# Operand addresses at multiples of 512 bytes, and the last three attention-branch panels after all gates

## The chip, the cores and the metric

The kernel runs on one core of a Trainium2 chip. The metric is the device time of one execution in microseconds (us). TensorE (PE) multiplies, VectorE (DVE), ScalarE (ACT) and GpSimd (POOL) work on tiles, and DMA queues, most of them issued from SyncE (SP), move data.

## The reference, cut to what matters

One block on 512 tokens of width 2048, all in float32:

```
h = rms_norm(x);  q, k, v, u, ga, gb = split(h @ w_in)         # 16 heads of 64
yA = chunked attention(q, k, v, clipped relative bias)         # width 1024
yB = multi-scale causal pooling(u) @ pool_w * pool_scale       # width 1024
m  = sigmoid(ga) * (yA @ w_branch_a) + sigmoid(gb) * (yB @ w_branch_b)
x1 = x + m @ w_out
out = rms_norm(x1 + (silu(g) * up) @ w_down),  g, up = split(rms_norm(x1) @ w_gate_up)
```

## The kernel before

**Precision.** A float32 operand is split in two float32r parts, a high part (an ACT copy) and a low part (a DVE subtraction). One product is three matmuls: low x high, high x high, high x low. A matmul has a stationary operand of 128 x 128 values (512 bytes in each partition), loaded by a LDWEIGHTS, and a moving one of 512 columns (2048 bytes in each partition; 256 columns for v).

**First half, panels.** `panel` (lines 204 to 206) computes 256 output columns of one weight matrix. Weights come in units of 4 x 256 columns: `load_to` issues the DMA into a `raw` tile (L143), `hi_to` splits off the high part on ACT (L152), `lo_to` the low part on DVE (L161); all three kinds lie in the pool `stage`, three tiles each. The unit is stationary, the activations move: `XH`/`XL` in the pool `xhl` (the normed input, 16 + 16 tiles), `ybh`/`ybl` and later `yah`/`yal` in the pool `mid`. In `panel_v` (L410 to L412) `XH`/`XL` are stationary and the weights move. Two more users of matmuls, pooling's small products and the attention scores, take both operands from the pool `slots`. The order is q, k, v, u, then the gb gates with the pooling-branch panels, then for i = 0 to 7 one ga gate panel ("g", 4 units) and one attention-branch panel ("y", 2 units). A unit is 24 matmuls. After a y panel, `evac_a` (L651, L652) makes 128 rows of the merged m twice and writes them to DRAM (L654).

**The seam.** After the last gate panel the tiles of `xhl` are given up; the pool `formsA` and two `half` tiles come in their place on the right side of the memory, and the generator `build_merged(fo, 0)` is put on the list `active`. It loads the first half of m (L736) and builds from it, in two halves, seven pairs of tiles `fP` (P1, P5, P6, P3, P7, P2, P4, in this order): ACT makes a high part (L724), DVE a low part (L727, L729), and for four of them DVE first makes the source (L716 to L719). Each `step()` moves every generator on `active` by one yield, and a panel has one step for each half unit, so a y panel has four. `drain()` then steps until nothing is left. After it the early pools are closed, and `formsB`, `raw2` (tile `r`) and `c` open on the left side over them, and other accumulators over the old ones.

**Second half, jobs.** `run_job` computes a block of w_out, w_gate_up or w_down by seven products for a 2 x 2 block matrix, in units of 512 columns; a job is 7 products x 2 units x 12 matmuls = 168 matmuls (L900 to L902), except the last two, which have 84. Forms are stationary, weights (`hiw`, `low` in `stage`) move. The first unit's weights of P1 are read straight from DRAM tiles; P5's need an addition on DVE (L849) of two of them, P6's another (L851). `load2_to` issues the DMAs (L828), `hi2_to` makes the high part on ACT (L863), `lo2_to` the low part on DVE (L871). Engines take their instructions strictly in the order in which this code gives them out. The order of jobs is o(0,0), o(0,1), o(1,0), o(1,1), eleven g(0,p), then eleven g(1,p) with d jobs between. Forms A serve 23 jobs: o(0,·), g(0,·) and d(0..4,·). Forms B serve o(1,·), g(1,·) and the two short ones d(5,·).

**Addresses.** A pool's tiles lie one behind the other. The left side starts at byte 2176 of each partition, the right side is filled downward from 229,344. Adding up the tiles gives:

| pool | side | start | start mod 512 |
|---|---|---|---|
| stage (raw, hi, lo; hiw, low) | left | 5,248 | 128 |
| formsB | left | 42,112 | 128 |
| slots | left | 47,520 | 416 |
| mid (yb, ya, and v for attention) | left | 111,200 | 96 |
| xhl, and later formsA | right, its upper end | 229,344 | 480 |

All tiles of these pools that a matmul reads are multiples of 512 bytes long, and all slices that it takes start at multiples of 512 bytes in them.

Of the kernel before, what the change touches and what calls it, by code (L numbers as in the profile page):

```python
# [10 lines left out]
F32 = mybir.dt.float32  # L11
# [5 lines left out]
P = 128  # L17
# [9 lines left out]
CU = 256  # L27
# [9 lines left out]
N_RAW2 = 6  # L37
N_C = 6
LOAD_AHEAD = 7

T_BY_DMA = False

# [2 lines left out]
def hybrid_block_kernel(  # L45
# [30 lines left out]
    KD = D // P  # L76
# [3 lines left out]
    KA = AW // P  # L80
# [6 lines left out]
    x = x[0]  # L87
    w_in, w_out, w_gate_up, w_down = w_in[0], w_out[0], w_gate_up[0], w_down[0]
    w_branch_a, w_branch_b, pool_w = w_branch_a[0], w_branch_b[0], pool_w[0]
    out = out[0]  # L90

    const = ctx.enter_context(tc.tile_pool(name="const", bufs=1))
    stage = ctx.enter_context(tc.tile_pool(name="stage", bufs=1))
    early = ctx.enter_context(ExitStack())
    const1 = early.enter_context(tc.tile_pool(name="const1", bufs=1))
    slots = early.enter_context(tc.tile_pool(name="slots", bufs=N_SLOTS))
    xtiles = ctx.enter_context(ExitStack())
    xhl = xtiles.enter_context(tc.tile_pool(name="xhl", bufs=2 * KD, side="right"))
    early_ps = ctx.enter_context(ExitStack())
    psum = early_ps.enter_context(tc.tile_pool(name="psum", bufs=1, space=bass.MemoryType.PSUM))  # L100
# [3 lines left out]
    def slot(dt=F32, name="t", pool=None):  # L104
        serial[0] += 1
        if pool is not None:
            return pool.tile([P, 512], dt, tag="b", name=f"{name}_{serial[0]}")
        return slots.tile([P, 512], dt, tag="t", name=f"{name}_{serial[0]}")
# [10 lines left out]
    def rows(w, r0, nk, c0, ncol):  # L119
        return w[r0:r0 + nk * P, c0:c0 + ncol].rearrange("(k p) c -> p k c", p=P)  # L120

    def add_panel(w, nk, c0, r0=0, cuts=None):
        k = 0
        for n in cuts or [KU] * (nk // KU):
            units.append((rows(w, r0 + k * P, n, c0, CU), n))
            k += n
        assert k == nk
# [51 lines left out]
    active, waiting, later = [], deque(), []  # L179
    since = [99]  # L180
    spacing = [6]

    def step():
        now, later[:] = list(later), []
        for fn in now:
            fn()
        since[0] += 1
        if waiting and since[0] >= spacing[0]:
            active.append(waiting.popleft())
            since[0] = 0  # L190
        for g in list(active):
            if next(g, "end") == "end":
                active.remove(g)
        for n in behind:
            lo_to(n)
            load_to(n + AHEAD)
        behind.clear()

    def drain():
        while active or waiting or later:  # L200
            step()
# [6 lines left out]
    def panel(nk, ah, al, evac, before=None, kind="d"):  # L208

        banks = [bank(kind), bank(kind)]  # L210
        k0, half = 0, 0
        while k0 < nk:
            hi, lo, n = next_unit()
            for oc in range(2):
                if before is not None:
                    before(half)
                half += 1
                for k in range(n):
                    kk = k0 + k
                    c = slice(oc * P, (oc + 1) * P)  # L220
                    product(banks[oc], hi[:, k, c], lo[:, k, c], ah[kk], al[kk], kk == 0, kk == nk - 1)
                step()
                if k0 + n == nk:
                    evac(oc, banks[oc])
            k0 += n
# [28 lines left out]
    GA, GB = 3 * AW + PWID, 3 * AW + PWID + D  # L254
    n_blk = D // CU
    b_order = [("g", 0), ("g", 1)] + [x for i in range(n_blk) for x in ((("y", i), ("g", i + 2)))]
    b_order = [x for x in b_order if x[1] < n_blk]
    for what, i in b_order:
        if what == "g":
            add_panel(w_in, KD, GB + i * CU)  # L260
        else:
            add_panel(w_branch_b, KB, i * CU)
    for i in range(n_blk):
        add_panel(w_in, KD, GA + i * CU)
        add_panel(w_branch_a, KA, i * CU)

    x_cols = [(0, 128), (128, 128), (256, 256), (512, 512), (1024, 512), (1536, 512)]
    xpool = ctx.enter_context(ExitStack())
# [9 lines left out]
    ident = const.tile([P, P], F32, name="ident")  # L278
    make_identity(nc, ident)
    warm = slot(mybir.dt.bfloat16, "warm")  # L280
    nc.vector.memset(warm, 0.0)
    ones = slot(F32, "ones")[:, :P]
    nc.vector.memset(ones, 1.0)
# [18 lines left out]

    XH, XL = [None] * KD, [None] * KD

    def turn_x(k):
# [3 lines left out]
        for t in range(NT):  # L309
            nc.tensor.transpose(ps[:, t * P:(t + 1) * P], xn[c][:, t, j:j + P], ident)  # L310
        XH[k], XL[k] = (xhl.tile([P, 512], F32R, tag="x", name=f"x{n}{k}") for n in "hl")
        xt = slot(F32, "xt")
        g = gains[:, k:k + 1]
        nc.scalar.activation(XH[k], ps, AF.Copy, scale=g)
        nc.scalar.activation(xt, ps, AF.Copy)
        nc.vector.scalar_tensor_tensor(XL[k], xt, g, XH[k].bitcast(F32), op0=ALU.mult, op1=ALU.subtract)

# [78 lines left out]
    def panel_v(i, pool):  # L396
# [3 lines left out]
        while k0 < KD:  # L400
            hi, lo, n = next_unit()
            for b in range(2):
                for k in range(n):
                    kk = k0 + k
                    for t in (2 * b, 2 * b + 1):
# [3 lines left out]
                        final = kk == KD - 1  # L409
                        mm(o, XH[kk][:, tok], hi[:, k], start=first, stop=False, skip_group_check=True)  # L410
                        mm(o, XH[kk][:, tok], lo[:, k], start=False, stop=False, skip_group_check=True)  # L411
                        mm(o, XL[kk][:, tok], hi[:, k], start=False, stop=final, skip_group_check=True)  # L412
# [149 lines left out]
    midpool = ctx.enter_context(ExitStack())  # L562
# [77 lines left out]
    def evac_gate(m, ps):  # L640
        SG[m] = slot(F32, "sg")
        nc.vector.tensor_tensor(SG[m], ps, r_bc, op=ALU.mult)
        nc.scalar.activation(SG[m], SG[m], AF.Sigmoid)
# [5 lines left out]
    def evac_a(m, ps):  # L649
        s = SG.pop(m)  # L650
        nc.vector.tensor_tensor(s, ps, s, op=ALU.mult)  # L651
        nc.vector.tensor_tensor(s, T.pop(m), s, op=ALU.add)  # L652
        m_dram[m] = tc.dram_tile([P, 512], F32, name=f"m_dram{m}")
        nc.gpsimd.dma_start(m_dram[m], s)  # L654
# [8 lines left out]
    YAH, YAL = {}, {}  # L663
# [11 lines left out]
    late = ctx.enter_context(ExitStack())  # L675
    pools = {}

    righted = ctx.enter_context(ExitStack())

    def forms_pool(which, side):  # L680
        pools[which] = (righted if side == "right" else late).enter_context(
            tc.tile_pool(name=f"forms{which}", bufs=1, side=side, reuse_waits="tile"))

    def new_forms(which):
        serial[0] += 1
        return {p: pools[which].tile([P, NPAIR, 2, 256], F32R, tag=f"f{p}", name=f"f{p}_{serial[0]}") for p in PRODUCTS}
# [44 lines left out]
    def build_merged(forms, kb):  # L731
        hs = []
        for h in range(2):
            half = yield from new_half()
            for j in range(4):
                nc.sync.dma_start(half[:, j // 2, j % 2], m_dram[8 * kb + 4 * h + j])  # L736
            hs.append(half)
            yield
        for h in range(2):
            yield from build(forms, h, hs[h])  # L740

    for i in range(n_blk):
        panel(KD, XH, XL, lambda oc, ps, i=i: evac_gate(2 * i + oc, ps))
        if i == n_blk - 1:
            XH = XL = None
            xtiles.close()
            forms_pool("A", "right")
            pools["half"] = righted.enter_context(tc.tile_pool(name="half", bufs=2, side="right", reuse_waits="tile"))
            fo = new_forms("A")
            active.append(build_merged(fo, 0))  # L750
            spacing[0] = 0
        panel(KA, YAH, YAL, lambda oc, ps, i=i: evac_a(2 * i + oc, ps))
    drain()
    midpool.close()
    early.close()
    early_ps.close()
    forms_pool("B", "left")
    rawp = late.enter_context(tc.tile_pool(name="raw2", bufs=N_RAW2, reuse_waits="tile"))
    cpools = [late.enter_context(tc.tile_pool(name="c", bufs=N_C, reuse_waits="tile"))]
    ps2 = late.enter_context(tc.tile_pool(name="psum2", bufs=1, space=bass.MemoryType.PSUM, reuse_waits="tile"))  # L760

    def ctile():
        serial[0] += 1
        return cpools[-1].tile([P, 2, 512], F32, tag="c", name=f"c_{serial[0]}")
# [58 lines left out]
    def load2_to(n):  # L823
        while loads and loads[0][0] <= n:
            _, j, q, h = loads.pop(0)
            t = rawtile(j, q, h)
            s, f = {"11": (0, 0), "12": (0, 1), "21": (1, 0), "22": (1, 1), "t1": (0, 0), "t3": (1, 1)}[q]
            nc.sync.dma_start(wide(t), j.quarter(s, f, h))  # L828
            if q[0] == "t":
                nc.gpsimd.dma_start(wide(t), j.quarter(0, 1, h), accum_op=ALU.add)  # L830
# [35 lines left out]
    def lo2_to(n):  # L866
        while st2["lo"] < min(n, len(wunits)):
            i = st2["lo"]
            hi2_to(i + 1)
            lo_t[-1 - i] = staged("lo", f"w{i}")  # L870
            nc.vector.tensor_tensor(lo_t[-1 - i], source(i), hi_t[-1 - i].bitcast(F32), op=ALU.subtract)  # L871
            st2["lo"] += 1
# [3 lines left out]
    def run_job(j):  # L876
# [3 lines left out]
        for n, p in enumerate(PRODUCTS):  # L880
# [8 lines left out]
            for h in range(j.nh):  # L889
                i = j.base + n * j.nh + h  # L890
                load2_to(i + LOAD_AHEAD)
                t_to(i + SPLIT + 1)
# [239 lines left out]
            Job(w_down, 8 * b, npair, p * 1024, p * 1024 + 512, None, d_done(b, p), acc)  # L1132
    plan_loads()

    o_forms = {0: fo}

    def build_o1():
# [2 lines left out]

    load2_to(LOAD_AHEAD - 2)
    lo2_to(SPLIT - 1)
# [50 lines left out]
```

## Time and profile before

| what | value |
|---|---|
| median of 3 runs (lowest, highest) | 2598.45 us (2597.3, 2599.5) |
| profiled execution: its own time; its span | 2599.56 us; 2597.7 us |
| PE, DVE, ACT busy, share of the span | 96%, 67%, 45% |
| mean granted TensorE clock | 0.988 |
| first half | to 1009 us |
| seam, no matmul | 1009.2 to 1030.0 us |
| jobs | 1030.0 us to the end |
| A jobs without a wait of PE between | 14, each 39.3 to 39.4 us |
| A jobs with such waits | 9, from 41.5 to 51.2 us |
| B jobs (long ones) with next to none | 6, from 38.15 to 38.9 us |
| B jobs (long ones) with waits | 7, from 44.9 to 47.2 us |

Matmuls overlap: a record of one lasts some 0.39 us, but the next one starts after 0.23 us. What a matmul costs is the distance between starts, so a stretch without a wait, divided by its number of matmuls. A window counts every record that touches it, so its count is one or two above the number of starts in it.

### The profile page before, as it was taken

The page shows a single profiled execution, that of the slowest core. Times are in us where ns is not written, and L with a number is a line of the kernel's source. Part 1 is how long each engine was busy: PE and PEld are TensorE (multiplying, and loading weights), DVE is VectorE, ACT ScalarE, POOL GpSimd, SP SyncE. Part 2 cuts the span into 40 slices and gives each one's busy share as a digit, 9 for nine tenths or more (in the row PEclk, how much of TensorE's full clock was granted, in tenths as well). Part 3 has the DMA queues.
Part 4 walks back from the last instruction along what each step waited for, and adds up shares of the span by engine and source line. Part 5 has one row for each costly group of instructions (what it writes and reads, how often), then busy time and mean ns, then how long its engine had stood idle before and what let it go on. Part 6 is the DMA issues. An engine that isn't in the chain of part 4 may idle for free.

```text
span 2597.7 us, 29053 instructions
## 1 busy us (share of the span) xinstructions
PE 2499.0 (96%) x11221; PEld 2007.5 (77%) x11221; DVE 1733.6 (67%) x1996; ACT 1163.7 (45%) x1499; POOL 151.4 (6%) x242
## 2 busy tenths in 40 slices
PE   9999999999999996999999999999999999999995
PEld 7888787888888885777788888877878778777773
DVE  6445556523243335878877777788887888879875
ACT  5444433322222222557544444455555555555554
POOL 0000000000000000110000000000100101001014
PEclk9999999999999998999999999999999999999997
DMA  5222232232333334583534435544654647537374
GB/s 172 94 86 86 73 93 86 85 98 92 95 105 104 112 104 167 147 249 122 192 114 180 179 121 187 190 118 134 158 178 108 192 119 181 172 104 196 100 207 121
DMA packets 203146, 352.20 MB, mean 136 GB/s; under 512 B 11304, under 2 KB 95856, under 8 KB 202880
## 3 DMA queue, kind: packets, MB, share of 16 engines
q1 hardware_dynamic: 177760, 263.76, 30.3%
q0 software_dynamic: 24096, 84.49, 13.9%
q8 instruction: 88, 1.44, 0.2%
q10 hardware_dynamic: 1152, 2.10, 0.2%
q14 instruction: 50, 0.41, 0.0%
HBM read 289.44 MB, written 60.86 MB: 135 GB/s over the span
## 4 chain that ended last, share of the span: by engine, by line
PE 85%; DVE 8%; issue 3%; ACT 2%; DMA 1%; ACTq 0%; SPq 0%; DVEq 0%; POOL 0%; POOLq 0%
PE psd L204 10%; PE psd L206 10%; PE psd L205 10%; PE psx L900 8%; PE psx L901 8%; PE psx L902 8%; PE psy L900 7%; PE psy L902 7%; PE psy L901 7%; DVE low L871 3%; DVE fP L727 1%; PE psd L410 1%; PE psd L412 1%; PE psd L411 1%; ACT hiw L863 1%
## 5 line engine op out<-in xcount | busy, mean ns | idle before, releaser
L871 DVE TENSOR_TENSOR low<-r,hiw 128x1024 fp32r<-128x1024 f32 x518 | 630.2, 1225 | 146.4 <-ACT hiw L863 145.2
L863 ACT ACTIVATE hiw<-r 128x1024 fp32r<-128x1024 f32 x518 | 546.4, 1057 | 390.2 <-PE psx L902 168.9
L900 PE MATMUL psx<-low,fP 128*128 128x512 f32 x1184 | 476.2, 402 | 48.5 <-DVE low L871 44.7
L902 PE MATMUL psx<-hiw,fP 128*128 128x512 f32 x1184 | 467.6, 395 | 0.0
L901 PE MATMUL psx<-hiw,fP 128*128 128x512 f32 x1184 | 467.5, 395 | 0.0
L161 DVE TENSOR_TENSOR lo<-raw,hi 128x1024 fp32r<-128x1024 f32 (+1 forms) x161 | 195.9, 1218 | 337.9 <-ACT hi L152 337.5
L900 PE MATMUL psy<-low,fP 128*128 128x512 f32 x888 | 355.8, 401 | 19.1 <-DVE low L871 17.3
L152 ACT ACTIVATE hi<-raw 128x1024 fp32r<-128x1024 f32 (+1 forms) x161 | 169.2, 1053 | 456.9 <-PE psd L206 338.6
L901 PE MATMUL psy<-hiw,fP 128*128 128x512 f32 x888 | 351.2, 395 | 0.0
L902 PE MATMUL psy<-hiw,fP 128*128 128x512 f32 x888 | 351.2, 395 | 0.0
L204 PE MATMUL psd<-xh,lo 128*128 128x512 f32 x864 | 345.0, 399 | 0.0
L206 PE MATMUL psd<-xl,hi 128*128 128x512 f32 x864 | 343.0, 397 | 0.0
L205 PE MATMUL psd<-xh,hi 128*128 128x512 f32 x864 | 340.9, 395 | 0.0
L900 PEld LDWEIGHTS psx<-low,fP 128*128 128x128 f32 x1184 | 223.2, 189 | 123.8 <-DVE low L871 69.0
L902 PEld LDWEIGHTS psx<-hiw,fP 128*128 128x128 f32 x1184 | 223.2, 189 | 52.4
L901 PEld LDWEIGHTS psx<-hiw,fP 128*128 128x128 f32 x1184 | 223.5, 189 | 47.0
L900 PEld LDWEIGHTS psy<-low,fP 128*128 128x128 f32 x888 | 167.9, 189 | 64.8 <-DVE low L871 18.6
L902 PEld LDWEIGHTS psy<-hiw,fP 128*128 128x128 f32 x888 | 168.0, 189 | 39.3
L901 PEld LDWEIGHTS psy<-hiw,fP 128*128 128x128 f32 x888 | 168.2, 189 | 36.2
L204 PEld LDWEIGHTS psd<-xh,lo 128*128 128x128 f32 x864 | 162.3, 188 | 40.8 <-issue 2.4
L206 PEld LDWEIGHTS psd<-xl,hi 128*128 128x128 f32 x864 | 162.2, 188 | 38.5
L205 PEld LDWEIGHTS psd<-xh,hi 128*128 128x128 f32 x864 | 162.4, 188 | 38.1
(207 smaller groups left out, 2813.2 us busy)
## 6 DMA issues: line engine op xcount, KB each, us to landing
r<-in_w_gate_up SPq DMA_DIRECT2D x176, 512.0 KB, 7.8
raw<-in_w_in SPq DMA_DIRECT2D x127, 512.0 KB, 3.7
r<-in_w_down SPq DMA_DIRECT2D x88, 512.0 KB, 6.7
x1d<-c POOLq DMA_DIRECT2D x48, 512.0 KB, 8.0
gp<-c POOLq DMA_DIRECT2D x44, 512.0 KB, 5.8
c<-gp POOLq DMA_DIRECT2D x33, 512.0 KB, 5.2
r<-in_w_out SPq DMA_DIRECT2D x32, 512.0 KB, 9.1
raw<-in_w_branch_b SPq DMA_DIRECT2D x16, 512.0 KB, 3.4
```

The costliest lines, as they stand in the source:

```text
L152: nc.scalar.activation(hi_t[i][:, :m], raw_t[i][:, :m], AF.Copy)
L161: nc.vector.tensor_tensor(lo_t[i][:, :m], raw_t[i][:, :m], hi_t[i].bitcast(F32)[:, :m], op=ALU.subtract)
L204: mm(ps, wl, ah, start=start, stop=False)
L205: mm(ps, wh, ah, start=False, stop=False)
L206: mm(ps, wh, al, start=False, stop=stop)
L410: mm(o, XH[kk][:, tok], hi[:, k], start=first, stop=False, skip_group_check=True)
L411: mm(o, XH[kk][:, tok], lo[:, k], start=False, stop=False, skip_group_check=True)
L863: nc.scalar.activation(hi_t[-1 - i], source(i), AF.Copy)
L871: nc.vector.tensor_tensor(lo_t[-1 - i], source(i), hi_t[-1 - i].bitcast(F32), op=ALU.subtract)
L900: mm(ps[:, t], fh, lo[:, k], start=first, stop=False, skip_group_check=True)
L901: mm(ps[:, t], fh, hi[:, k], start=False, stop=False, skip_group_check=True)
L902: mm(ps[:, t], fl, hi[:, k], start=False, stop=last, skip_group_check=True)
```

## The change

Four unused tiles are added, as padding: 384 bytes ahead of `const`, 224 ahead of `const1`, 320 behind the slots, and 480 at the right end. The start of `stage` is then 5,632, of `slots` 48,128, of `mid` 112,128, of `formsB` 42,496, and the upper end of the right side 228,864: all five are multiples of 512.

The order of the last stage of the first half changes: for i = 0 to 4 a gate and a y panel as before, then gates 5, 6, 7, then y panels 5, 6, 7. `build_merged(fo, 0)` is put on `active` after gate 7, now three y panels ahead of the end. At the start of the last y panel the first two w_out tiles are loaded and the first is split; the second is split after the panel, ahead of `drain()`.

```diff
+PAD_CONST, PAD_CONST1, PAD_SLOTS, PAD_RIGHT = 96, 56, 80, 120
+N_TAIL = 3
...
+    const.tile([P, PAD_CONST], F32, name="pad")
+    const1.tile([P, PAD_CONST1], F32, name="pad1")
+    padr = ctx.enter_context(tc.tile_pool(name="padr", bufs=1, side="right"))
+    padr.tile([P, PAD_RIGHT], F32, name="pad2")
+    slots.tile([P, PAD_SLOTS], F32, tag="pad3", name="pad3", bufs=1)
...
-    for i in range(n_blk):
-        add_panel(w_in, KD, GA + i * CU)
-        add_panel(w_branch_a, KA, i * CU)
+    a_order = [x for i in range(n_blk - N_TAIL) for x in (("g", i), ("y", i))]
+    a_order += [(what, i) for what in "gy" for i in range(n_blk - N_TAIL, n_blk)]
+    for what, i in a_order:
+        if what == "g":
+            add_panel(w_in, KD, GA + i * CU)
+        else:
+            add_panel(w_branch_a, KA, i * CU)
...
+    for what, i in a_order:
+        if what == "g":
+            panel(KD, XH, XL, lambda oc, ps, i=i: evac_gate(2 * i + oc, ps))
+            if i == n_blk - 1:
+                XH = XL = None
+                xtiles.close()
+                forms_pool("A", "right")
...
+                fo = new_forms("A")
+                active.append(build_merged(fo, 0))
+                spacing[0] = 0
+        else:
+            if i == n_blk - 1:
+                load2_to(1)
+                lo2_to(1)
+            panel(KA, YAH, YAL, lambda oc, ps, i=i: evac_a(2 * i + oc, ps))
+    lo2_to(2)
+    drain()
+    midpool.close()
```

The jobs are planned ahead of this loop instead of behind it, so that `load2_to` and `lo2_to` can be called in it.

## Rows read from the trace of the kernel before

**Rows 1.** The page: busy time of engines; one group of matmuls, with its count

```profile
PE 2499.0 (96%) x11221; PEld 2007.5 (77%) x11221; DVE 1733.6 (67%) x1996; ACT 1163.7 (45%) x1499; POOL 151.4 (6%) x242
...
L204 PE MATMUL psd<-xh,lo 128*128 128x512 f32 x864 | 345.0, 399 | 0.0
```

**Rows 2.** Windows: length, busy us (instructions) by engine, granted clock, DMA share, GB/s

```profile
500.00:920.00 420.00, 420.00 (x1801) 338.04 (x1801) 137.88 (x144) 98.46 (x109) 5.44 (x10) 1.00 0.32 101
63.58:86.24 22.66, 22.66 (x192) 22.66 (x191) 10.67 (x14) 9.47 (x14) 0.00 (x0) 1.00 0.30 93
...
1451.83:1491.20 39.37, 39.37 (x169) 31.64 (x168) 29.64 (x26) 18.52 (x18) 2.13 (x4) 1.00 0.46 168
1648.66:1686.81 38.15, 38.15 (x169) 31.31 (x168) 28.94 (x26) 20.90 (x21) 3.16 (x4) 1.00 0.64 192
```

**Rows 3.** Windows of line L410 alone: busy us (instructions) of PE, then weight loads

```profile
26.00:1009.00 983.00, 72.90 (x256) 48.24 (x256) 1.00 0.31 96
```

**Rows 4.** Timeline of PE in one pooling product, first and last matmul: start, us

```profile
410.92 0.39 PE L204 MATMUL psa<-dh,pwl 128*128 128x512 f32 x1
...
412.08 0.40 PE L206 MATMUL psa<-dl,pwh 128*128 128x512 f32 x1
```

**Rows 5.** Waits of PE, seam first, then 1201 us on: total us, times, longest

```profile
PE psx L900 <- DVE low L871: 20.9, 1, 20.9
...
PE psx L900 <- DVE low L871: 20.3, 29, 1.1
```

**Rows 6.** Timeline of PE at the seam: last y, four of P1 and P5

```profile
1008.77 0.40 PE L206 MATMUL psd<-yal,hi 128*128 128x512 f32 x1
1030.03 0.79 PE L900 MATMUL psx<-low,fP 128*128 128x512 f32 x1 [20.86 <-DVE low L871]
...
1031.05 0.63 PE L902 MATMUL psx<-hiw,fP 128*128 128x512 f32 x1
...
1034.89 0.61 PE L902 MATMUL psx<-hiw,fP 128*128 128x512 f32 x1
...
1038.15 0.40 PE L900 MATMUL psy<-low,fP 128*128 128x512 f32 x1
```

**Rows 7.** Timeline of DVE at the seam

```profile
1009.93 0.69 DVE L652 TENSOR_TENSOR sg<-sg,sg 128x512 f32<-128x512 f32 x1
...
1012.65 0.69 DVE L729 SCALAR_TENSOR_TENSOR fP<-s,fP 128x512 fp32r<-128x512 f32 x1 [0.70 <-ACT fP L724]
...
1017.36 1.89 DVE L727 TENSOR_TENSOR fP<-half,fP 128x512 fp32r<-128x512 f32 x3
...
1028.75 2.36 DVE L871 TENSOR_TENSOR low<-r,hiw 128x1024 fp32r<-128x1024 f32 x2
1031.03 2.36 DVE L849 TENSOR_TENSOR r<-r,r 128x1024 f32<-128x1024 f32 x2
1033.46 1.23 DVE L871 TENSOR_TENSOR low<-r,hiw 128x1024 fp32r<-128x1024 f32 x1
```

**Rows 8.** The w_out DMAs at the seam: SP's last three issues; time to landing

```profile
1007.79 1.53 SPq L828 DMA_DIRECT2D r<-in_w_out  x3
...
DMA to landing us min/median/max: 4.1/6.3/7.7
```

**Rows 9.** Windows around the seam: columns as in Rows 2

```profile
1009.20:1030.00 20.80, 0.00 (x0) 0.00 (x0) 15.67 (x24) 9.45 (x15) 0.54 (x1) 0.55 0.45 151
1030.00:1036.00 6.00, 5.97 (x15) 4.71 (x16) 5.83 (x5) 1.48 (x2) 0.00 (x0) 0.55 0.95 336
1036.00:1074.45 38.45, 37.09 (x154) 28.43 (x153) 34.48 (x38) 21.81 (x27) 5.36 (x6) 1.00 0.62 162
```

**Rows 10.** Windows of single jobs with waits: g(0,0), g(1,1), d(0,0); columns as in Rows 2

```profile
1201.33:1252.55 51.22, 46.11 (x201) 35.58 (x200) 44.45 (x49) 35.50 (x62) 2.13 (x4) 0.97 0.39 148
1686.81:1731.80 44.99, 41.52 (x185) 32.72 (x184) 40.02 (x42) 25.63 (x32) 2.51 (x3) 1.00 0.52 148
1776.71:1818.75 42.04, 41.28 (x185) 33.11 (x184) 33.98 (x31) 20.88 (x23) 2.58 (x3) 1.00 0.37 102
```

More of the change, by code (lines that the diff above doesn't have):

```diff
@@ L740, in build_merged @@
             yield from build(forms, h, hs[h])
[L742 to L760, printed above, removed]
     def ctile():
@@ L1133, in hybrid_block_kernel @@
     plan_loads()
+    for what, i in a_order:
[5 more added lines that the diff above has]
+                forms_pool("A", "right")
+                pools["half"] = righted.enter_context(
+                    tc.tile_pool(name="half", bufs=2, side="right", reuse_waits="tile"))
+                fo = new_forms("A")
[9 more added lines that the diff above has]
+    midpool.close()
+    early.close()
+    early_ps.close()
+    forms_pool("B", "left")
+    rawp = late.enter_context(tc.tile_pool(name="raw2", bufs=N_RAW2, reuse_waits="tile"))
+    cpools = [late.enter_context(tc.tile_pool(name="c", bufs=N_C, reuse_waits="tile"))]
+    ps2 = late.enter_context(tc.tile_pool(name="psum2", bufs=1, space=bass.MemoryType.PSUM, reuse_waits="tile"))
     o_forms = {0: fo}
```

## The prediction

> **What bounds the kernel now.** I read the page's busy shares first. TensorE is busy for 96% of the span, VectorE for 67% [rows 1], so the time is the number of matmuls times their distance, plus what TensorE waits. Second come windows in which TensorE never waits [rows 2]. From 500 to 920 us it starts some 1,800 matmuls of 512 columns (the count of 1,801 holds one or two that only touch the edges): 420 us by 1,800 is 233.3 ns each. In the panel of v, with 256 columns, it is 22.66 by 191, 118.6 ns. Two jobs, each of 168 matmuls by the code, differ: 39.37 us with forms A, 234.3 ns each, and 38.15 us with forms B, 227.1 ns each. The clock is granted in full in all four (1.00, the 2.4 GHz level), both jobs run the same lines on the same weight tiles, and VectorE has some 30 us of work in each, well under the job's length. What differs is the pool that the stationary operand comes from. By the table of addresses, forms B and the weights both start 128 bytes past a multiple of 512; forms A start 480 past one. In the panels the stationary weights are at 128 and the moving tiles at 480 (x) or at 96 (yb, ya): again one operand that is no multiple of 64, and again 233. So I read the 6 to 7 ns as the price of an operand that starts 32 bytes off a multiple of 64, or of two that differ by that.
>
> Third, the waits [rows 5]. The longest is 20.9 us at the seam, for VectorE; the waits for `low` in the jobs are many and short (29 of one kind come to 20.3 us). The chain at the seam stands in VectorE's order: the last evacuation, the forms of the second half-build, then `low` for the first weights [rows 7].
>
> **Part 1: addresses.** Nothing is computed otherwise; 1,536 bytes or less are lost on a side, and no tile has to move to another pool. I take the distance of every matmul whose operands are now at 480, 96 or 416 to be that of forms B.
>
> *Panels.* Each of lines 204 to 206 runs 864 matmuls on x [rows 1] and 128 each on yb and ya by the code (8 panels x 2 units x 8): 3 x 1,120 = 3,360. At 233.3 - 227.1 = 6.2 ns each that is 20.8 us. In this half VectorE and ScalarE are idle for two thirds of the time (137.88 and 98.46 of 420 us) and the weights need 101 GB/s, so nothing else becomes late.
>
> *v.* 3 x 256 matmuls [rows 3], from 118.6 to half of 227.1, 113.6: 5.0 ns, 3.9 us.
>
> *Jobs on forms A.* 14 run without a wait, each worth 39.37 - 38.15 = 1.22 us: 17.1 us. Nine have waits; there VectorE is the slower one for part of the job. d(0,0) has 34.0 us of VectorE work in 42.0, g(0,0) 44.5 in 51.2 [rows 10]. I give them 0.7 us each, 6.3 us, between 0 (all given back in new waits) and 1.22 each (11.0). Jobs on forms B keep their distance; those with waits, as the one at 1686.81 with 40.0 us of VectorE work in 45.0, are not shortened by faster matmuls at all.
>
> The sum is 48.1 us. Its ends: nothing, if the pools differ by something else than the address, and more, if 128 past a multiple of 512 has a price too. Both are rivals below.
>
> **Part 2: the order at the seam.** Call the end of the last y panel T; before it was at 1009.0 (the last matmul starts at 1008.77 and the next would have been 0.23 later), the first matmul of P1 at 1030.03, of P5 at 1038.15 [rows 6], so P5 at T+29.15. Matmuls, splits, stores and DMAs are the same in number; what changes is what lies beside what.
>
> The generator now meets 12 steps ahead of T, not four. It yields twice for its loads, then once for each form. After 12 steps all seven forms of the first half-build and P1, P5 of the second are done, and P6's high part and source; P6's low part, P3, P7, P2 and P4 are left to `drain()`. At T VectorE still has, in order: the last evacuation, to T+1.6 (before it ended at 1009.93 + 0.69); `low` of the second unit, 1.2 (half of 2.36); and the rest of the forms. Before, the same row of work ran from 1012.65 to two thirds through the group that begins at 1017.36, 1018.65: 6.0 us, most of it VectorE and ScalarE waiting for each other in turn. That makes T+8.9. Then P5's two additions and its first `low`, 1031.03 to 1034.69 before, 3.7 us: T+12.6 [rows 7].
>
> P1 itself no longer waits for that: its forms and first unit are ready, its accumulators are free at the latest when the last evacuation is, T+1.6, and the second unit's `low` is there at T+2.9. Its 24 matmuls end near T+7. So TensorE waits some 1 us, works 5.5, and waits 5.6 for P5: the wait of 20.9 is not removed but becomes two, and the second is late by VectorE's order. P5 comes at T+12.6, 16.5 us sooner.
>
> Against that stands the clock. After the 20.8 us without a matmul the grant was at 0.55 until 1036 [rows 9], that is mostly at 1.2 GHz: 15 starts in 5.97 us in place of 15 x 0.234 = 3.5, a loss of 2.4. Before, that loss lay in P1; now, if a wait of 5.6 us brings the clock down too, it lies in P5. Bounds: no loss, 16.5 us gained; all 24 matmuls of P5 at half speed, 4.7 lost, 11.8 gained. I take the 2.4 of the row: 14.1 us. VectorE is busy for 34.5 of the 38.5 us after 1036, so part of it could be hidden in that and part of part 1 in o(0,0) lost; I leave both.
>
> *Queues.* SP: the second half of m waits for the last reader of x, which is now 22 us sooner against T; the w_out tiles follow it. Three of them were issued only from 1007.79, 1.2 us ahead of T, since `r` lies over tiles that the last y panel reads; with 7.7 us at most to landing that is T+6.5, ahead of the additions at T+8.9 [rows 8]. POOL: six stores of m more fall close together at the end, all needed only by the next build. ScalarE: the first high part of w_out waits for a slot that the panel before gives back at the start of the last panel; behind it are only form copies, nothing TensorE needs in that panel. The first form's copy waits for the last gate matmul as it did. The three gates in a row hold six gate tiles in place of two, in a ring of 31 of which 16 hold the other branch. No matmul waits for any of these; if one did, it would be for the unit at the head, 5.6 us at most.
>
> **The sum.** 20.8 + 3.9 + 17.1 + 6.3 + 14.1 = 62.2 us off the profiled execution's 2599.56 is 2537.4. The median is 1.1 lower, so the forecast is 2536 us. With the smallest and largest value of the unsettled terms (the nine jobs 0 to 11.0, the seam 11.8 to 16.5) and half a nanosecond on the distance, its own range is 2524 to 2550.
>
> **Rivals.**
>
> *Multiples of 512 are better than forms B.* The pooling products speak for a price by degrees: both operands are at 416, so do not differ, and still their starts are (412.08 - 410.92) / 5 = 232 ns apart [rows 4]. So the address itself counts, and 128 may not be free. How far down it could go: at 1.2 GHz nine starts take 1034.89 - 1031.05 = 3.84 us, 427 ns each [rows 6], one column per clock; the same at 2.4 GHz would be 213. Take 220, about half way: panels 44.7, v 6.6, 14 A jobs 33.6, nine A jobs half, 10.8, six B jobs without waits 7.2, seam 14.1: 117 us, 2481. Against it: no row shows a matmul of 512 columns in a steady stream under 227. The Trainium skill (TensorE: Matmul & The Clock Gate, Back-to-back issue gap) gives 512 columns 216 ns when warm; no run here shows that, the rows are 11 to 18 ns above it.
>
> *The address does nothing.* Forms A lie at the far end of the memory, forms B next to the weights; x and ya are far from the weights as well. If distance or the pool's place is the price, padding by some hundred bytes changes no matmul, and only the seam is left: 2584. The pooling products, near to each other and slow, speak against it. The Trainium skill (SBUF — State Buffer, Who interferes with whom) says that TensorE waits for no one at the memory and has separate reads for both operands; by that rule this rival holds, and the two jobs of 39.37 and 38.15 us disagree with it.
>
> *The seam stays as long.* If form copies in ScalarE's order wait for loads of m, and weight splits for the last y panels stand behind them, the wait is only moved into the panels. Then 48.1 us alone: 2550. Against it: the loads of m were issued while the last gate still ran.
>
> *Slower.* Two streams that start at the same multiple of 512 might meet in the same part of the memory at every step. The slowest rate that rows show is that of v, 237.3 ns for 512 columns. On 8,232 matmuls without waits (3,360 in panels, 3,864 on forms A, 1,008 on forms B) the seam's 14.1 us are used up at a mean distance of 234.7; at 237.3 the kernel takes 21 us more than before, about 2620. Against it: forms B and the weights already start at the same place in 512 and are the fastest.
>
> **How the numbers follow.** Forecast 0.55, better than forms B 0.20, no effect of the address 0.13, seam as long 0.08, slower 0.04. The range 2478 to 2587 leaves out the better part of the first rival (0.09), the worse part of the second (0.04) and the slower case. A difference under 0.2%, 5.2 us, can't be told from none here; only the second rival with a poor seam ends there, 0.03. Faster 0.93, slower 0.04.
>
> **What would show it.** The window from 500 to 920 should hold some 1,850 matmuls; every unwaited job some 38.15 us, on either forms; v's panel 21.7 us. The one wait of 20.9 us should be two, the longer near 6 us and in front of P5, with VectorE's `low` as its releaser; the granted clock around it tells who is right on the 2.4 us. A and B jobs that still differ, or a distance under 225 ns, would make the forecast wrong.

## The result, and the profile after

The changed kernel takes 2540.82 us (2539.93 to 2542.43) against 2598.52 us beside it, a ratio of 0.9779 (0.9762 to 0.9796): 57.7 us faster. The forecast was 2536. The profiled execution's span is 2539.5 us, 58.2 less than before.

Windows of the changed kernel, with the columns of [rows 2]: the panels, the panel of v, one of the jobs on forms A, one on forms B, and the three jobs with waits of [rows 10], which are g(0,0), g(1,1) and d(0,0).

```profile
500.00:920.00 420.00, 420.00 (x1854) 347.90 (x1853) 142.88 (x149) 102.12 (x113) 5.44 (x10) 1.00 0.33 103
61.56:84.46 22.90, 22.90 (x193) 22.90 (x191) 10.72 (x14) 9.51 (x14) 0.00 (x0) 1.00 0.29 95
1371.67:1409.77 38.10, 38.10 (x169) 31.32 (x168) 29.63 (x26) 18.53 (x18) 2.14 (x4) 1.00 0.44 162
1600.27:1638.37 38.10, 38.10 (x169) 31.32 (x168) 29.07 (x26) 20.92 (x21) 3.16 (x4) 1.00 0.66 197
...
1165.37:1216.23 50.86, 45.60 (x201) 35.49 (x200) 44.36 (x49) 35.27 (x62) 2.13 (x4) 0.97 0.40 148
1638.37:1683.39 45.02, 41.55 (x185) 32.71 (x184) 40.04 (x42) 25.64 (x32) 2.51 (x3) 1.00 0.51 149
1728.33:1769.55 41.22, 40.39 (x185) 32.80 (x184) 33.81 (x31) 20.90 (x23) 2.58 (x3) 1.00 0.37 99
```

The same 420 us hold 1,854 matmuls in place of 1,801, and jobs on both forms are equally long: 38.10 us, 226.8 ns a matmul. The panel of v is not shorter but longer, 22.90 us in place of 22.66. The job g(1,1) at 45.0 us, on forms B and with 40 us of VectorE work, kept its length, as forecast.

The seam: TensorE's waits from 975 to 1050 us, then its timeline (last y matmul, first of P1, first of P1's second unit, last of P1, first of P5).

```profile
PE psy L893 <- DVE low L864: 6.8, 2, 6.5
PE psx L893 <- DVE low L864: 3.2, 5, 1.5
```

```profile
987.57 0.39 PE L213 MATMUL psd<-yal,hi 128*128 128x512 f32 x1
987.80 0.39 PE L893 MATMUL psx<-low,fP 128*128 128x512 f32 x1
...
990.95 0.50 PE L893 MATMUL psx<-low,fP 128*128 128x512 f32 x1 [0.28 <-DVE low L864]
...
993.58 0.39 PE L895 MATMUL psx<-hiw,fP 128*128 128x512 f32 x1
1000.43 0.79 PE L893 MATMUL psy<-low,fP 128*128 128x512 f32 x1 [6.46 <-DVE low L864]
```

VectorE's timeline of the changed kernel shows what P5 waited for: last evacuation, second split, rest of the forms, P5's additions and its split.

```profile
988.72 0.69 DVE L665 TENSOR_TENSOR sg<-sg,sg 128x512 f32<-128x512 f32 x1
989.67 1.23 DVE L864 TENSOR_TENSOR low<-r,hiw 128x1024 fp32r<-128x1024 f32 x1 [0.26 <-ACT hiw L856]
990.81 0.69 DVE L742 SCALAR_TENSOR_TENSOR fP<-s,fP 128x512 fp32r<-128x512 f32 x1
...
995.52 1.29 DVE L740 TENSOR_TENSOR fP<-half,fP 128x512 fp32r<-128x512 f32 x2
996.73 2.35 DVE L842 TENSOR_TENSOR r<-r,r 128x1024 f32<-128x1024 f32 x2
999.15 1.23 DVE L864 TENSOR_TENSOR low<-r,hiw 128x1024 fp32r<-128x1024 f32 x1
```

The one wait of 20.9 us [rows 5] became one of 6.5 with the same releaser. Windows over that wait, over P5 at the low clock, and from P5 to the next job (columns as before) show the clock. The fourth line is the kernel before, from its P5 to its next job.

```profile
993.81:1000.43 6.62, 0.16 (x1) 0.00 (x0) 5.82 (x8) 3.96 (x6) 0.00 (x0) 0.91 0.80 284
1000.43:1006.07 5.64, 5.64 (x13) 4.46 (x14) 5.61 (x6) 2.38 (x4) 1.28 (x1) 0.50 1.00 311
1000.43:1039.07 38.64, 36.82 (x144) 28.66 (x145) 35.44 (x39) 20.98 (x26) 5.35 (x6) 0.93 0.71 192
...
1038.15:1074.45 36.30, 34.94 (x145) 26.73 (x144) 33.04 (x37) 21.17 (x26) 5.36 (x6) 1.00 0.62 157
```

Where the 58.2 us came from, by the starts of matmuls in both traces: T moved from 1009.0 to 987.8, 21.2 us; from T to the second job 65.46 us became 51.28, 14.2 us; from there to the end 22.8 us.

### The profile page after: what moved, and what is told of

Read it like the earlier page. It is cut to its first block, busy times and chain, and to the rows that moved or that the text cites. A ratio compares the mean times of both kernels' runs of the same rounds, so it can differ in the third digit from the quotient of the medians.

```text
span 2539.5 us, 29049 instructions
## 1 busy us (share of the span) xinstructions
PE 2455.2 (97%) x11221; PEld 2002.9 (79%) x11221; DVE 1732.6 (68%) x1996; ACT 1163.4 (46%) x1499; POOL 151.3 (6%) x242
## 3 DMA queue, kind: packets, MB, share of 16 engines
q0 software_dynamic: 24096, 84.49, 14.2%
## 4 chain that ended last, share of the span: by engine, by line
PE 86%; DVE 8%; issue 3%; ACT 2%; DMA 1%; ACTq 0%; SPq 0%; POOL 0%; DVEq 0%; POOLq 0%
PE psd L211 10%; PE psd L212 10%; PE psd L213 10%; PE psx L893 8%; PE psx L894 8%; PE psx L895 8%; PE psy L893 7%; PE psy L895 7%; PE psy L894 7%; DVE low L864 3%; PE psd L423 1%; DVE fP L740 1%; PE psd L425 1%; PE psd L424 1%; ACT hiw L856 1%
## 5 line engine op out<-in xcount | busy, mean ns | idle before, releaser
L213 PE MATMUL psd<-xl,hi 128*128 128x512 f32 x864 | 336.7, 390 | 0.0
```

The costliest lines, as they stand in the source:

```text
L213: mm(ps, wh, al, start=False, stop=stop)
```

## The experiments

All are edits of the changed kernel except the first, which edits the kernel before. Each ratio is to the kernel before, run beside it.

**1. The paddings alone**

```diff
+    const.tile([P, PAD_CONST], F32, name="pad")
...
+    const1.tile([P, PAD_CONST1], F32, name="pad1")
...
+    padr.tile([P, PAD_RIGHT], F32, name="pad2")
...
+    slots.tile([P, PAD_SLOTS], F32, tag="pad3", name="pad3", bufs=1)
```

> The kernel before with the four paddings alone. If the two parts of the change add up, as my account of the two traces says (21.2 us in the first half, 23.0 us after the first job), this run takes 2598.5 - 44 = 2554 us: matmuls of 512 columns 226.7 ns apart in panels and in jobs on both forms, and the wait of 20.9 us at the seam unchanged. Rival: the new order is what speeds up the matmuls of the first half, too; then 2575 or more.

Measured: 2552.63 us, 0.9826 (0.981 to 0.9843). Windows of TensorE alone (length, busy us and count, clock, DMA share, GB/s), panels and then jobs on forms A, and the longest wait at the seam:

```profile
500.00:920.00 420.00, 420.00 (x1855) 1.00 0.33 102
1300.00:1600.00 300.00, 300.00 (x1324) 1.00 0.45 164
```

```profile
PE psx L907 <- DVE low L878: 21.9, 3, 20.9
```

The matmuls have all of their gain and the seam none of it: 45.3 us belong to the addresses.

**2. The new order alone**

```diff
-    const.tile([P, PAD_CONST], F32, name="pad")
...
-    const1.tile([P, PAD_CONST1], F32, name="pad1")
...
-    padr.tile([P, PAD_RIGHT], F32, name="pad2")
...
-    slots.tile([P, PAD_SLOTS], F32, tag="pad3", name="pad3", bufs=1)
```

> The changed kernel without the four paddings. If the parts add up, 2598.5 - 14 = 2584 us, with 233.3 ns in the panels, 234.3 in jobs on forms A, 227 on forms B, and a wait of some 6.5 us ahead of P5 in place of 20.9 ahead of P1. Rival: slower matmuls in P1 let VectorE catch up, the wait falls under 5 us and the clock stays up; then 2580 or less.

Measured: 2585.43 us, 0.9948 (0.9933 to 0.9963). The same windows, and the wait:

```profile
500.00:920.00 420.00, 420.00 (x1801) 1.00 0.33 100
1300.00:1600.00 300.00, 300.00 (x1283) 1.00 0.46 168
```

```profile
PE psy L887 <- DVE low L858: 6.4, 1, 6.4
```

The panels are as slow as before, so the order does nothing to them. The order alone is worth 12.5 us; 45.3 + 12.5 = 57.8, against 57.7 for both together: the parts add up.

**3. The padding at the right end alone**

```diff
-    const.tile([P, PAD_CONST], F32, name="pad")
...
-    const1.tile([P, PAD_CONST1], F32, name="pad1")
...
-    slots.tile([P, PAD_SLOTS], F32, tag="pad3", name="pad3", bufs=1)
```

> The changed kernel with the padding at the right end alone: x and forms A start at a multiple of 512, the weights stay at 128 past one, yb and ya at 96, slots at 416. Theory A, each operand counts by its own start and a multiple of 64 is enough: x panels and all jobs 226.7 ns, only the 768 matmuls on yb and ya stay at 233.3, together about 2546 us. Theory B, the two operands must start at the same place in 512: x panels and forms A stay at 233 to 234, about 2584 us. Theory C, both must be at multiples of 512: at best half of the gain, about 2560 us. Theory D, distance or pool and not the address: 2584 us.

Measured: 2577.12 us, 0.9919 (0.99 to 0.9939). Panels, jobs on forms A, one job on forms B:

```profile
500.00:920.00 420.00, 420.00 (x1806) 1.00 0.33 100
1300.00:1600.00 300.00, 300.00 (x1293) 1.00 0.46 169
1627.27:1665.38 38.11, 38.11 (x169) 1.00 0.65 192
```

x and forms A now start at a multiple of 512, the weights at a multiple of 128, and still the matmuls stand some 232.4 ns apart in both, 1 ns less than before on x and 2 ns less on forms A. A multiple of 64 on both sides is not enough: theory A falls, and it was mine. No theory gave 2577; B, with 2584, is the nearest.

**4. Every pool 32 bytes past a multiple of 512**

```diff
-PAD_CONST, PAD_CONST1, PAD_SLOTS, PAD_RIGHT = 96, 56, 80, 120
+PAD_CONST, PAD_CONST1, PAD_SLOTS, PAD_RIGHT = 104, 56, 80, 112
```

> The changed kernel with every pool at 32 past a multiple of 512, so that the two operands of every matmul start at the same place. Theory B (only the difference counts): 226.7 ns throughout and 2541 us. Theory A (each operand's own start): about 232 ns, as pooling's products at 416 and 416 had it before, on 8,200 unwaited matmuls 5 ns each, about 2580 us.

Measured: 2539.83 us, 0.9776 (0.9756 to 0.9796), as the changed kernel. The same three windows:

```profile
500.00:920.00 420.00, 420.00 (x1855) 1.00 0.34 103
1300.00:1600.00 300.00, 300.00 (x1324) 1.00 0.45 162
1599.42:1637.50 38.08, 38.08 (x169) 1.00 0.66 196
```

This is the run that decides. No operand starts at a multiple of 64, let alone 512, and every class of 512 columns stands at 226.7 ns. What counts is that both operands start at the same place.

**5 and 6. Other differences**

```diff
-    const.tile([P, PAD_CONST], F32, name="pad")
...
-    const1.tile([P, PAD_CONST1], F32, name="pad1")
...
+    padb.tile([P, PAD_B], F32, name="padb")     # ahead of formsB
...
-PAD_CONST, PAD_CONST1, PAD_SLOTS, PAD_RIGHT = 96, 56, 80, 120
+PAD_SLOTS, PAD_RIGHT, PAD_B = 24, 24, 112      # run 5
+PAD_SLOTS, PAD_RIGHT, PAD_B = 48, 80, 16       # run 6
```

> The changed kernel with other paddings: the weights at 128 past a multiple of 512, x and forms A at 384 (256 from the weights), yb and ya at 192 (64 from them), forms B at 64 (64 from them on the other side). Theory B (only the same start in 512 bytes is fast): none of the four is, about 232 to 234 ns on x, on yb and ya and in jobs on both forms, so that jobs on forms B without a wait take some 39 us and the whole some 2587 us. Theory E (the pattern repeats every 256 bytes): x and forms A at 226.7. Theory F (it repeats every 64 bytes, and 32 apart was the fault): all at 226.7 and 2541 us; the run with the right end alone speaks against F already.

> The changed kernel with a third set of paddings, to fill in the differences not yet seen (start of the moving operand less start of the stationary one, modulo 256): 32 on x, 224 with forms A, 160 on yb and ya, 192 with forms B. Theory E (the pattern repeats every 256 bytes; 0 is the best, 64 and 192 next at 229, the odd multiples of 32 and 128 at 232 to 234): x 233, jobs on forms A 39.2 us, yb and ya 233, jobs on forms B 38.5 us, together about 2581 us. Rival: some other difference is better than 0, since at 0 every matmul still takes 13 ns longer than its 512 columns at 2.4 GHz; then one of the four is under 226 ns.

Measured: 2547.55 us, 0.9804 (0.9783 to 0.9826), and 2588.47 us, 0.9965 (0.9949 to 0.998). Panels, jobs on forms A, one job on forms B, of run 5 and then of run 6:

```profile
500.00:920.00 420.00, 420.00 (x1845) 1.00 0.33 102
1300.00:1600.00 300.00, 300.00 (x1324) 1.00 0.44 163
1603.72:1642.22 38.50, 38.50 (x169) 1.00 0.66 195
```

```profile
500.00:920.00 420.00, 420.00 (x1800) 1.00 0.33 100
1300.00:1600.00 300.00, 300.00 (x1288) 1.00 0.46 169
1631.83:1671.04 39.21, 39.21 (x169) 1.00 0.63 188
```

In run 5 x and forms A are 256 bytes from the weights and fast: theory E, not B, though I had expected B's 2587. Forms B, fast in every kernel so far, are slowed in both: to 38.5 us in run 5 and 39.2 in run 6. The 192 of run 6 was expected at 229 and came at 233, so the pattern is not symmetric. The table gives all differences seen (start of the moving operand less that of the stationary one, modulo 256; only multiples of 32 occur) and the mean distance of starts of matmuls of 512 columns in stretches without a wait:

| difference | ns | where |
|---|---|---|
| 0 | 226.7; 227 | run 4, changed kernel; x and forms A of run 5 (256 apart) |
| 32 | 233.3 | x of run 6 |
| 64 | 229.2 | yb, ya and forms B of run 5 |
| 96 | 233.3 | x of the kernel before |
| 128 | 232.4 | x and forms A of run 3 |
| 160 | 234.3; 234.1 | forms A before; yb, ya of run 6 |
| 192 | 233.3 | forms B of run 6 |
| 224 | 233.4; 233.3 | yb, ya before; forms A of run 6 |

Classes with one difference agree to 0.4 ns, whichever operand is the stationary one and wherever in the memory they lie; 0 is the best of the eight. That 256 bytes apart is as good as 0 is shown by x and forms A of run 5; in run 3 the moving operand starts 128 bytes below the stationary one on x and 128 above it on forms A, and both stand at 232.4.

These are distances in long stretches. Behind a stretch with another difference some matmuls can pass before they are reached. In the kernel before, the job that starts at 1648.67 has difference 0 and follows one with 160; these are its first, sixth and ninth matmul:

```profile
1648.67 0.39 PE L900 MATMUL psx<-low,fP 128*128 128x512 f32 x1
...
1649.83 0.39 PE L902 MATMUL psx<-hiw,fP 128*128 128x512 f32 x1
...
1650.51 0.39 PE L902 MATMUL psx<-hiw,fP 128*128 128x512 f32 x1
```

The first five distances take 1.16 us, 232 ns each, the next three 0.68, 227 each.

**7. Four y panels behind the gates**

```diff
-N_TAIL = 3
+N_TAIL = 4
```

> The changed kernel with four y panels behind all gates in place of three, so that the build of forms has 16 steps ahead of the end of the last panel and only one low part is left to drain. If the 6.5 us wait ahead of P5 is VectorE's remaining row of form work, as I say, it goes down to some 1.3 us (evacuation, one split, one low part, 3.7 us for P5's additions and split, against P1's end at T+6.0), the clock is not lowered, and the kernel takes 5.3 + 2.5 = 7.8 us less than the changed one, 2533 us. Rival: P5's weights, whose second tile is issued only 1.4 us ahead of T, are late next and land at T+3 to T+6, so that P5 waits 2 to 3 us for the DMA; then about 2535. Rival: the wait is kept up by something else than the forms; then 2541.

Measured: 2533.01 us (2531.05 to 2533.46), 0.9747 (0.9732 to 0.9762), the best of all. Waits at the seam, then windows from the end of P1 to P5, over the whole first job, and from P5 to the second job:

```profile
PE psx L893 <- DVE low L864: 1.6, 3, 0.6
PE psy L893 <- DVE low L864: 1.5, 2, 1.2
```

```profile
994.54:995.87 1.33, 0.17 (x1) 0.00 (x0) 1.24 (x2) 1.26 (x3) 0.00 (x0) 1.00 1.04 413
...
988.88:1031.92 43.04, 39.96 (x169) 30.98 (x168) 41.99 (x46) 23.28 (x28) 5.90 (x7) 1.00 0.85 265
...
995.87:1031.92 36.05, 34.13 (x144) 26.74 (x145) 35.35 (x39) 20.98 (x26) 5.36 (x6) 1.00 0.82 248
```

P5 starts at T+7.0 (expected 7.3), the granted clock stays at 1.00, and the first job is 8.2 us shorter than in the changed kernel: 5.6 of it ahead of P5, and 2.6 behind it (36.05 us against 38.64), where the clock was low. VectorE works 42.0 of its 43.0 us: it is now the bound there. The waits for P5 (`psy`) end with VectorE and not with a DMA, so the DMA rival falls.

**8. No early split**

```diff
-            if i == n_blk - 1:
-                load2_to(1)
-                lo2_to(1)
...
-    lo2_to(2)
     drain()
```

> The changed kernel without the loads and splits of the first two w_out units ahead of drain. The build of forms then ends at T+7.7 in place of T+8.9 (one split less ahead of it), two high and two low parts follow, and P1 starts near T+10, P5 a little after its own split, near T+16; 3 to 4 us more than the changed kernel, about 2544 us, with one wait of some 10 us in front of P1 and the clock lowered in P1. Rival: since P5 waits for VectorE's row of work whatever lies ahead, the place of the early split costs nothing; then 2541.

Measured: 2542.4 us, 0.9784 (0.9767 to 0.9802). Timeline of TensorE (last y, first of P1, first of P5), and the window over P1.

```profile
987.76 0.39 PE L213 MATMUL psd<-yal,hi 128*128 128x512 f32 x1
996.89 0.79 PE L893 MATMUL psx<-low,fP 128*128 128x512 f32 x1 [8.73 <-DVE low L864]
...
1005.22 0.39 PE L893 MATMUL psy<-low,fP 128*128 128x512 f32 x1
```

```profile
996.90:1005.20 8.30, 8.30 (x24) 6.59 (x25) 7.40 (x7) 2.12 (x2) 0.00 (x0) 0.65 0.88 309
```

P1 starts 8.9 us behind T, P5 at T+17.2, 4.6 later than with the early split. But the low clock then lies in P1 (0.65) and not in P5, and the second job starts at T+53.1 against T+51.3: 1.8 us. In the medians it is 1.6, less than the 2.5 us by which runs of the changed kernel alone lie apart. Both expectations miss: the early split is worth less than 3 us, and the runs don't show that it is worth nothing.

## Why the prediction was right, and where its reason was wrong

**Panels.** Forecast 20.8 us. The mean distance fell by 6.0 ns on the 2,592 matmuls on x and by 6.7 on the 768 on yb and ya, which makes 20.7. Right.

**v.** Forecast +3.9 us, measured -1.0: 118.6 ns became 120.0. This is the step that failed, by 4.9 us: more than the 4.0 us by which the sum (62.2) was too high against the traces (58.2). Against it stand 1.5 us that the first half gained elsewhere, in shorter waits and small products, which the forecast left out. I halved the distance of 512 columns. At difference 0 the distance is 226.7 for 512 columns and 120.0 for 256. My estimate for one column per clock at 2.4 GHz, half of the 427 ns of [rows 6], is 213.3 and 106.7, and both lie some 13.3 ns above it. At difference 0, then, it looks like a price per matmul and not per column, and halving was wrong. At difference 160, in the kernel before, the two lie 21 and 12 ns above it (234.3 and 118.6), and halving nearly held.

**Jobs.** The 14 without waits were forecast at 1.22 us each and gave 1.25 on average (1.20 to 1.27). The waiting ones gave 0.35 to 0.82 us each, o(0,0) apart, against 0.7 forecast. From the second job to the end 22.8 us came off; the forecast had 17.1 + 8 x 0.7 = 22.7. Right. No job behind the first became longer by more than 0.04 us.

**The seam.** P5 came at T+12.6, as forecast (the terms 1.6 + 1.2 + 6.0 + 3.7 add up to 12.5). VectorE's order explains it, and run 7, which takes most of that row of work away, brings the wait down to 1.3 us. P1 came at T and not at T+1.6, so that the wait of TensorE for P5 was 6.6 us and not 5.6. The clock came down in that wait and cost 38.64 - 36.30 = 2.3 us against the kernel before, and 2.6 against run 7, whose matmuls are as fast and whose clock stayed up; forecast 2.4. From T to the second job 14.2 us came off; the forecast had 14.1 and 0.7 for o(0,0).

**The reason for the 6 to 7 ns.** The prediction offered two readings in one sentence, an operand off a multiple of 64 or two operands that differ, and argued with the first. Run 4 excludes it. Runs 3, 5 and 6 show the second in a wider form: differences of 64, 128 and 192 cost something too, not only odd multiples of 32. That the forecast came out all the same is partly luck in the choice: starts at multiples of 512 serve either reading, because they are also equal starts. The rival of something better than forms B fails: forms B before were already at difference 0. So does the slower rival, whose premise, the same start, is the fastest case for 512 columns; its 8,232 matmuls "without waits" also counted the nine jobs on forms A with waits.

The pooling product at 416 and 416, which I took as a sign for the first reading, has difference 0 and still stood at 232. The trace of the kernel before shows why: the product has only six matmuls, behind a panel with another difference, and its five distances take the same 1.16 us as the first five of the job that starts at 1648.67 (experiments 5 and 6), which stands at 227 from there on. In run 6, with the slots still at 416, the first and last matmul of the same product are 1.14 us apart, 228 ns each, so 416 has no such price of its own:

```profile
409.15 0.39 PE L209 MATMUL psa<-dh,pwl 128*128 128x512 f32 x1
...
410.29 0.40 PE L211 MATMUL psa<-dl,pwh 128*128 128x512 f32 x1
```

Six matmuls were too few to read a distance from.

The Trainium skill (SBUF — State Buffer, Who interferes with whom) has TensorE waiting for no one, with separate reads for the two operands. The runs show a dependence that this rule does not provide for: the distance goes by where the two operands lie to each other, 226.7 to 234.3 ns.

**What would have shown it.** From 500 to 920 us the forecast named 1,850 matmuls (1,854 counted) and 38.15 us for every unwaited job (38.10 on both forms). It named 21.7 us for v's panel, which came at 22.90.

## What to carry to other kernels

Where every float32r matmul loads new weights and has 512 moving columns, give the stationary and the moving operand the same start modulo 256; paddings of a few hundred bytes gave 45 us of 2598 here, and no multiple of 512 is needed. To find such a thing, compare the distance of starts between long stretches that run the same lines without a wait but from other pools. When a chain is moved ahead of a wait, follow the engine's order on to the next consumer: here the wait moved from P1 to P5 with a third of its length, and one more panel (run 7) took all but 1.3 us of it away.

## What the hardware showed that was not expected

The distance of two matmuls depends on the difference of the operands' starts, with a period of 256 bytes (0 and 256 alike, 227), and not evenly: 64 costs 2.5 ns, 128 costs 5.7, the others 6.6 to 7.6. For 256 columns it is the other way round: the panel of v has 120.0 ns at difference 0, 118.6 before, at 160, and 118.3 in run 6, at 128 - 160 = -32, that is 224 (22.60 us by 191):

```profile
62.24:84.84 22.60, 22.60 (x193) 1.00 0.31 93
```

The distance also depends on what ran just before: the job that starts at 1648.67 needed five matmuls to settle. Which part of the chip makes all this so, no run shows.
